# The second layer's modulation vectors as VectorE dot products in the first layer's feed-forward part, in place of fp32 matrix products in its attention part

## The chip, the cores and the metric

One core of one Trainium2 chip runs the whole program, which is launched once. The metric is the device time of that core in microseconds, a median over runs. Engines are named as in the profile: PE is TensorE's matrix product, PEld its weight load, DVE is VectorE, ACT is ScalarE, SP is SyncE, whose queue issues all the DMAs of this kernel.

## What is computed

Two blocks of two layers each run one after the other on 256 tokens of width 1024 in fp32. The change lies in the first block, a diffusion-style transformer with a second stream of 256 context tokens. Per layer, a conditioning vector is turned into six modulation vectors of 1024 numbers, once for the tokens (from `c`) and once for the context (from `c_ctx`):

```python
silu_c, silu_cc = silu(c), silu(c_ctx)
for l in range(2):
    mod_x = silu_c  @ w_ada[l] + b_ada[l]        # w_ada[l]: 1024 x 6144
    mod_c = silu_cc @ w_ada[l] + b_ada[l]
    sh1, sc1, gt1, sh2, sc2, gt2 = split(mod, 6)  # of each
    h = rms_norm(x, g1) * (1 + sc1) + sh1          # tokens and context
    ... three kinds of attention on h @ w_in ...
    x = x + gt1 * (concat(oa, ob, oc) @ w_out[l])
    h2 = rms_norm(x, g2) * (1 + sc2) + sh2
    x = x + gt2 * conv_ffn(h2)
    # the context is updated in the same way, in layer 0 only
```

In layer 1 the context only gives keys and values, so of its six vectors only sh1 and sc1 are used there.

## The kernel before, in words

Products of activations with weights are made of three fp32r products (`mm3`, L175 to L180): each operand is split into a high and a low half, and high by high, high by low and low by high are added up in PSUM. A weight piece of 128x1024 is loaded as `wraw` (L144), copied to a high half `wh` by ACT (L259), and DVE subtracts to get the low half `wl` (L260). PE needs both halves, so PE waits for DVE when DVE is behind.

The modulation of a layer is `ada(l)` (L305). It works in 24 steps: 3 groups of 2048 outputs, 8 steps of 128 rows of `w_ada` each. A step loads two pieces of 128x1024 and makes four plain fp32 products of 128x512 (L318) with the conditioning columns as the stationary operand; four of the 128x32 column groups of PE are used, one for each 512 outputs. After 8 steps DVE adds the bias (L323), PE transposes the row to columns (`ada_cols`, L343), DVE copies the columns out, and the two groups with gates are written to DRAM, from where `gate_rows` (L365) reads each gate back as a row for all partitions.

`ada` is a generator. `tick` (L336) takes one step of it, and `layer` (L747) calls `tick` at the products with `w_in` (`chunk`, L771) and once per head or head pair in the attention (L599, L646). In layer 0 the generator is `ada(0)` followed by `ada(1)` (L754): 8 steps of `ada(0)` run before the first norm, and the other 16 of `ada(0)` and all 24 of `ada(1)` during the attention; what is left is taken at L844.

Layer 0 then goes on: out-projection (`out_proj`, L722), the norm of both streams (`norm_to`, L843), and the feed-forward part (L847 to L864). That has three parts of 8, 7 and 7 hidden tiles. `ffn_up` (L705) makes one tile: two weight pieces, 48 products of 128x512, a convolution of three taps on ACT (L698) and DVE (L701, L702, once for each of two halves), a gate (L716, L717) and a split (L259, L260). Then the down-projection of the part runs, in two halves of the output, with DVE adding the gated result to `x` (L681, L682).

A scheduler decides where each instruction stands on its engine: the order of the source gives it priorities, and independent instructions are moved forward into places where an engine would wait. So the `ada` products stand between the score and output products of the attention. Each engine then runs its own list strictly in order.

Of the kernel before, what the change touches and what calls it, by code (L numbers as in the profile page):

```python
# [12 lines left out]
F32 = mybir.dt.float32  # L13
# [37 lines left out]
class Core:  # L51
    def __init__(self, ctx, tc):
# [20 lines left out]
                  ta32=(64, 4), tb32=(64, 4), nlam=(1, 2), gsubs=(64, 2), raw=(512, 3), rpb=(512, 1), bada=(512, 1))  # L73
# [208 lines left out]
class Block1:  # L282
# [52 lines left out]

    def tick(self):  # L336
        next(self.side, None)
# [21 lines left out]
    def gate_rows(self, l, n, s):  # L359

        K = self.K
        out = K.xo()
        for j in range(2):
            a = 2 * (2 * (n - 1) + j) + s
            self.nc.sync.dma_start(out[:, j * 512 : j * 512 + 512], self.rows[l, n][a : a + 1, :].to_broadcast([P, 512]))  # L365
        return out
# [380 lines left out]
    def layer(self, l):  # L747
# [5 lines left out]
        if l == 0:  # L753
            self.side = chain(*(self.ada(i) for i in range(self.depth)))  # L754
            front = [K.normed(self.x[0]), None]
            for _ in range(KD):
                self.tick()
        else:
            front = [None, None]
# [87 lines left out]
        if full:  # L847
            parts = [range(0, 8), range(8, 15), range(15, 22)]
            for part in parts:
                F = {}  # L850
                for j in part:
                    F[j] = self.ffn_up(l, j, XT, n)
                for cc in range(2):
                    ps = K.acc4()
                    for a in range(part[0], part[-1] + 1, 4):
                        nf = min(4, part[-1] + 1 - a)
                        get = K.weights(f"w1_{l}", "w_down", l, a, nf, [cc * 512], 512)
                        for t in tts:
                            for f in range(nf):
                                j = a + f  # L860
                                K.mm3(ps[t], (F[j][0][:, t * P : t * P + P], F[j][1][:, t * P : t * P + P]), get(f * 512, 512),
                                      j == part[0], j == part[-1])
                    for t in tts:
                        self.add_gated(self.x[t // 2][t % 2][:, cc * 512 : cc * 512 + 512], ps[t], gates[t // 2][:, cc * 512 : cc * 512 + 512])  # L864
        else:
# [592 lines left out]
def _pack(inputs, specs):  # L1458
# [10 lines left out]
    for key, layer, k0, nk, starts, width, piece in specs:  # L1469
        if (key, layer) not in done:  # L1470
            w = inputs["w_in_2" if key == "w_kr_2" else key][layer]
# [63 lines left out]
```

## Time and profile before

| | before |
|---|---|
| median of 3 runs | 2169.36 us (2168.35 to 2172.04) |
| the profiled execution's own time | 2168.22 us |
| span in its trace | 2166.4 us |
| PE busy | 2081.5 us, 96% |
| PEld busy | 1850.0 us, 85% |
| DVE busy | 1493.9 us, 69% |
| ACT busy | 1075.5 us, 50% |
| mean granted TensorE clock | 0.978 of 2.4 GHz |

By stage of layer 0 in the trace: the attention with its products with `w_in` from 34 to 327 us, the out-projection to 377, the norm to 396, the feed-forward part to 757. Layer 1 of the first block has its attention from 832 to 938 us. The busy time of an engine is a union of its instructions; a window's number in brackets is a count of instructions. "PEclk" is the mean clock that was granted in the stretch, as a share of 2.4 GHz.

### The profile page before, as it was taken

Reading aid. Unit: us, or ns where it says so; the run is one execution under the profiler, and the core shown is the slowest. Engines: PE = TensorE matmul, PEld = TensorE weight load, DVE = VectorE, ACT = ScalarE, POOL = GpSimd, SP = SyncE. Lnnn points to the kernel's source line nnn. Section 1 sums busy time; section 2 is a strip of 40 time slices with the busy share of each in tenths; the row PEclk is TensorE's granted clock in tenths of the full one; section 3 lists DMA queues with packets and bytes.
Section 4 is the critical chain, followed back from the end, with each engine's and each line's share of the span. In section 5 each row is a group of like instructions: output and inputs, shape, how many; then the busy total and the mean of one; then the engine's idle time right before and its main releaser. Section 6 shows DMA issues by size and latency. Waiting matters only on the chain.

```text
span 2166.4 us, 35861 instructions
## 1 busy us (share of the span) xinstructions
PE 2081.5 (96%) x14228; PEld 1850.0 (85%) x14228; DVE 1493.9 (69%) x3008; ACT 1075.5 (50%) x1837; POOL 0.8 (0%) x7
## 2 busy tenths in 40 slices
PE   6999999899999999989999999989998999998998
PEld 3886859688888898879997899979997899997997
DVE  5664666755555688687778799775556879876554
ACT  4545552542424366656556644454445644454443
POOL 0000000000000000000000000000000000000000
PEclk9999999899999999999999999999999999999999
DMA  8345563414142321145553555645553455654552
GB/s 341 122 164 180 202 218 116 156 58 146 55 138 67 128 89 55 39 135 199 197 190 132 165 178 182 196 156 171 189 185 123 156 166 163 197 187 139 188 183 72
DMA packets 94840, 331.65 MB, mean 153 GB/s; under 512 B 10928, under 2 KB 11312, under 8 KB 94544
## 3 DMA queue, kind: packets, MB, share of 16 engines
q1 hardware_dynamic: 94672, 329.35, 45.8%
q8 instruction: 112, 1.84, 0.3%
q14 instruction: 56, 0.46, 0.1%
HBM read 328.20 MB, written 1.11 MB: 152 GB/s over the span
## 4 chain that ended last, share of the span: by engine, by line
PE 90%; DVE 6%; ACT 2%; DMA 1%; issue 1%; DVEq 0%; ACTq 0%
PE ps L178 17%; PE ps L179 17%; PE ps L180 17%; PE acc L178 6%; PE acc L179 6%; PE acc L180 6%; PE ada L318 3%; PE ps L525 2%; PE o L566 2%; PE ps L550 2%; PE ada L180 1%; PE ada L178 1%; PE ada L179 1%; PE o L178 1%; PE o L179 1%; PE o L180 1%
## 5 line engine op out<-in xcount | busy, mean ns | idle before, releaser
L178 PE MATMUL ps<-T,wh 128*128 128x256 f32 (+1 forms) x2640 | 787.6, 299 | 1.1 <-ACT T L262 1.1
L179 PE MATMUL ps<-T,wh 128*128 128x256 f32 (+1 forms) x2640 | 785.6, 298 | 0.4 <-DVE T L263 0.4
L180 PE MATMUL ps<-T,wl 128*128 128x256 f32 (+1 forms) x2640 | 784.6, 298 | 0.0
L260 DVE TENSOR_TENSOR wl<-wraw,wh 128x1024 fp32r<-128x1024 f32 (+1 forms) x514 | 608.5, 1200 | 151.0 <-ACT wh L259 83.7
L259 ACT CAST wh<-wraw 128x1024 fp32r<-128x1024 f32 (+1 forms) x514 | 515.9, 1032 | 236.7 <-PE ps L179 77.3
L178 PEld LDWEIGHTS ps<-T,wh 128*128 128x128 f32 x2640 | 506.2, 192 | 18.5 <-ACT T L262 2.2
L179 PEld LDWEIGHTS ps<-T,wh 128*128 128x128 f32 x2640 | 506.5, 192 | 17.3 <-DVE T L263 1.2
L180 PEld LDWEIGHTS ps<-T,wl 128*128 128x128 f32 x2640 | 506.2, 192 | 13.7
L178 PE MATMUL acc<-wh,T 128*128 128x256 f32 (+1 forms) x988 | 314.9, 320 | 4.3 <-ACT T L265 3.1
L179 PE MATMUL acc<-wl,T 128*128 128x256 f32 (+1 forms) x988 | 313.6, 318 | 1.9 <-DVE wl L260 1.9
L180 PE MATMUL acc<-wh,T 128*128 128x256 f32 (+1 forms) x988 | 312.0, 317 | 0.3 <-DVE T L269 0.3
L178 PEld LDWEIGHTS acc<-wh,T 128*128 128x128 f32 x988 | 191.5, 194 | 20.9 <-ACT T L265 3.5
L180 PEld LDWEIGHTS acc<-wh,T 128*128 128x128 f32 x988 | 190.7, 193 | 14.6 <-DVE arena L268 1.7
L179 PEld LDWEIGHTS acc<-wl,T 128*128 128x128 f32 x988 | 191.4, 194 | 13.0 <-DVE wl L260 2.4
L1132 DVE SCALAR_TENSOR_TENSOR arena<-arena 128x241 f32<-128x241 f32 (+14 forms) x240 | 113.1, 473 | 3.7
L259 ACT CAST T<-arena 128x256 fp32r<-128x256 f32 (+2 forms) x128 | 58.8, 468 | 96.2 <-PE ps L179 25.8
L534 DVE TENSOR_REDUCE arena<-ps 128x1 f32<-128x512 f32 (+1 forms) x100 | 67.0, 683 | 44.9 <-PE ps L525 44.5
L318 PE MATMUL ada<-wraw,arena 128*32 128x512 f32 x384 | 86.5, 622 | 11.0 <-DVE arena L293 8.4
L1340 DVE TENSOR_TENSOR arena<-arena,ps 128x256 f32<-128x256 f32 x44 | 18.5, 421 | 113.8 <-ACT arena L1339 113.8
L260 DVE TENSOR_TENSOR T<-arena,T 128x256 fp32r<-128x256 f32 (+2 forms) x128 | 63.1, 500 | 48.6 <-ACT T L259 48.2
L698 ACT ACTIVATE arena<-ps,arena 128x512 f32<-128x512 f32 (+1 forms) x88 | 58.8, 669 | 74.6 <-PE ps L180 74.6
L1339 ACT ACTIVATE arena<-ps 128x256 f32<-128x256 f32 x44 | 16.9, 384 | 156.4 <-PE ps L180 156.4
(226 smaller groups left out, 2316.1 us busy)
## 6 DMA issues: line engine op xcount, KB each, us to landing
wraw<-w SPq DMA_DIRECT2D x586, 512.0 KB, 4.1
wraw<-w SPq DMA_DIRECT2D x22, 256.0 KB, 3.4
xo<-row SPq DMA_DIRECT2D x12, 256.0 KB, 5.7
v<-xin SPq DMA_DIRECT2D x4, 512.0 KB, 7.9
arena<-rpb SPq DMA_DIRECT2D x8, 256.0 KB, 3.5
v<-post SPq DMA_DIRECT2D x4, 512.0 KB, 4.0
arena<-bada SPq DMA_DIRECT2D x6, 256.0 KB, 6.9
arena<-bc SPq DMA_DIRECT2D x2, 768.0 KB, 4.0
```

The costliest lines, as they stand in the source:

```text
L178: mm(out, ah, bh, start=start, stop=False)
L179: mm(out, ah, bl, start=False, stop=False)
L180: mm(out, al, bh, start=False, stop=stop)
L259: a = nc.scalar.copy(h, src)
L260: b = nc.vector.tensor_tensor(l, src, h.bitcast(F32), op=ALU.subtract)
L318: nc.tensor.matmul(ps[32 * g : 32 * g + 32, :], self.cT[:, k].rearrange("p s r -> p (s r)"), raw[g // 2][0][:, g % 2 * 512 : g % 2 * 512 + ...
L525: self.nc.tensor.matmul(ps[:, col : col + 256], a[:, c], b, start=(n == 0), stop=(n == len(q[s]) - 1))
L534: nc.vector.tensor_reduce(m, ps.rearrange("p (t k) -> p t k", t=nt), axis=AX, op=ALU.max, negate=True)
L550: nc.tensor.transpose(ps[:, b * P : b * P + P], p[:, b * P : b * P + P], K.ident)
L566: self.nc.tensor.matmul(out[64 * i : 64 * i + 64, t * P : t * P + P], v[:, k, cols[i] : cols[i] + 64], pts[i][:, b * P : b * P + P], start ...
L698: nc.scalar.activation(y[:, :n], ps[:, :n], AF.Identity, scale=cw[:, j, 1:2], bias=self.sm["cb"][:, j : j + 1])
L1132: yield v.scalar_tensor_tensor(y[:, lo:hi], zs[j][:, lo + t - 15 : hi + t - 15], self.cfw[:, j, t : t + 1], y[:, lo:hi], op0=ALU.mult, op1 ...
```

## The change

Layer 1's modulation is no longer made by `ada`. `w_ada[1]` is sent transposed, so that an output stands on a partition and its 1024 weights lie along the free axis. `crows` loads the two conditioning vectors as one row pair for all partitions (1 MB) and takes their silu on ACT. `ada_dots` has 48 steps, one for each 128 outputs: a step loads one piece of 128x1024, and DVE multiplies it by the conditioning row and sums along the row in one instruction (`scalar_tensor_tensor` with `accum_out`; the product itself goes to a tile `unread`). For sh1 and sc1, the first 16 steps, it does so twice, once for each stream, for the others once: 64 such instructions. After each 8 steps a small add puts the bias on, and for the scales the gain. The two gates are written to DRAM as columns and read back as one row each.

The steps are ticked in layer 0's feed-forward part: two after each up-tile, one after each half of a down-projection, 50 places for 48 steps. `ada(0)` stays as it was, and its 16 later steps still run in the attention.

```diff
-                  ta32=(64, 4), ..., raw=(512, 3), rpb=(512, 1), bada=(512, 1))
+                  ta32=(64, 4), ..., raw=(512, 3), rpb=(512, 1), bada=(512, 1), badac=(48, 1), adav=(48, 2), crow=(2048, 1), unread=(1024, 1))
...
+    def crows(self):
+        K, nc = self.K, self.nc
+        self.crow = K.tile([P, 2, D], F32, "crow")
+        nc.sync.dma_start(self.crow, self.ap["crow"].partition_broadcast(P))
+        nc.scalar.activation(self.crow, self.crow, AF.Silu)
+        self.badac = K.tile([P, 48], F32, "badac")
+        nc.sync.dma_start(self.badac, self.ap["badac"])
...
+    PARTS = dict(sh1=0, sc1=8, gt1=16, sh2=24, sc2=32, gt2=40)
+    def ada_dots(self, l):
...
+        vals = [K.tile([P, 48], F32, "adav") for _ in range(2)]
+        for name, b0 in self.PARTS.items():
+            streams = (0, 1) if name in ("sh1", "sc1") else (0,)
+            for b in range(b0, b0 + 8):
+                ((w, _),) = K.raw(f"w1_{l}", "w_ada_t", l, b, 1, [0], D)
+                for s in streams:
+                    nc.vector.scalar_tensor_tensor(K.tile([P, D], F32, "unread"), w, 1.0, self.crow[:, s], op0=ALU.mult, op1=ALU.mult,
+                                                   accum_out=vals[s][:, b : b + 1])
+                if b == b0 + 7:
+                    for s in streams:
+                        self.part(l, name, s, vals[s][:, b0 : b0 + 8], self.gn[:, l])
+                yield
+    def part(self, l, name, s, v, gn):
...
+        nc.vector.tensor_tensor(v, v, self.badac[:, b0 : b0 + 8], op=ALU.add)
+        if name[:2] == "gt":
+            row = self.rows[l, int(name[2])] = K.dram.tile([1, D], F32, name=f"row_{l}_{name}_{s}")
+                nc.sync.dma_start(row.rearrange("o (b p) -> p (o b)", p=P), v)
+            return
...
     def gate_rows(self, l, n, s):
+        if l > 0:
+            self.nc.sync.dma_start(out, self.rows[l, n].to_broadcast([P, D]))
+            return out
...
         if l == 0:
-            self.side = chain(*(self.ada(i) for i in range(self.depth)))
+            self.side = self.ada(0)
...
         if full:
+            self.crows()
+            self.side = self.ada_dots(l + 1)
             parts = [range(0, 8), range(8, 15), range(15, 22)]
...
                     F[j] = self.ffn_up(l, j, XT, n)
+                    self.tick()
+                    self.tick()
...
+                    self.tick()
                     for t in tts:
                         self.add_gated(...)
+            for _ in self.side:
+                pass
```

Lines move with the new code. In the lists of the changed kernel below, L359 is the new dot product, L572, L597 and L691 are the scores, transposes and outputs of the attention (L525, L550 and L644 before), L748, L749 and L764 the convolution and gate of an up-tile (L701, L702 and L717 before).

PE's list in the last attention of layer 0 (`attend_c`), before. `ada` are the modulation products, `o` and `ps` the attention's.

```order
L318 MATMUL ada_2498<-wraw_2991,arena 32x512 x2
L550 MATMUL ps_2908<-arena 128x128 x4
L644 MATMUL o_2917<-v_294_2838,arena 128x64 x4
L550 MATMUL ps_2940<-arena 128x128 x4
L318 MATMUL ada_2498<-wraw_3020,arena 32x512
L644 MATMUL o_2917<-v_294_2838,arena 128x64 x4
```

The same place of the changed kernel; `acc` are sums of the out-projection, which stood behind the attention before.

```order
L178 MATMUL acc_3170<-wh_3175,T_2141 128x256
L179 MATMUL acc_3170<-wl_3176,T_2141 128x256
L180 MATMUL acc_3170<-wh_3175,T_2141 128x256
L691 MATMUL o_2823<-v_271_2744,arena 128x64 x4
L178 MATMUL acc_3170<-wh_3175,T_2141 128x256
L572 MATMUL ps_2920<-T_2752,T_2536 128x256
L572 MATMUL ps_2920<-T_2778,T_2536 128x256
```

In the places that the `ada` products left, the scheduler put products of later stages; in the first attention of this stretch (`attend_ab`) these are the products of the next `w_in` chunk. Some 135 such products stand inside `attend_c` now, and some 73 inside `attend_ab`.

DVE's list in the norm before the feed-forward part, before: the end of the first stream's splits (L268, L269), and the scaling (L232) of the second stream's last tile.

```order
L269 TENSOR_TENSOR T_3914<-arena,T_3914 128x256
L201 SCALAR_TENSOR_TENSOR arena<-arena 128x1
L355 SCALAR_TENSOR_TENSOR arena<-ps_4074,arena 128x8
L202 SCALAR_TENSOR_TENSOR arena<-arena 128x1
L965 TENSOR_SCALAR arena<-arena 128x124
L232 TENSOR_SCALAR xo_3986<-v_310_2901,arena 128x512
```

The same place of the changed kernel:

```order
L359 SCALAR_TENSOR_TENSOR arena<-wraw_4016,arena 128x1024
L269 TENSOR_TENSOR T_3712<-arena,T_3712 128x256
L200 SCALAR_TENSOR_TENSOR arena<-arena 128x1
L359 SCALAR_TENSOR_TENSOR arena<-wraw_4020,arena 128x1024
L201 SCALAR_TENSOR_TENSOR arena<-arena 128x1
L359 SCALAR_TENSOR_TENSOR arena<-wraw_4020,arena 128x1024
L202 SCALAR_TENSOR_TENSOR arena<-arena 128x1
L232 TENSOR_SCALAR xo_3784<-v_287_2807,arena 128x512
```

Five dot products now stand in the norm: two between the first stream's scalings and its splits, and these three ahead of the last scaling of the second stream. Three more stand ahead of the norm, among the out-projection's adds, and one ahead of the norm's last split.

DVE's list in the first part of up-tiles, before: two convolutions, a gate, a split of a tile and two weight splits.

```order
L701 SCALAR_TENSOR_TENSOR arena<-ps_4172,arena 128x2x255
L702 SCALAR_TENSOR_TENSOR arena<-ps_4172,arena 128x2x255
L260 TENSOR_TENSOR T_4157<-arena,T_4157 128x512
L260 TENSOR_TENSOR wl_4315<-wraw_4308,wh_4314 128x1024
L260 TENSOR_TENSOR wl_4384<-wraw_4379,wh_4383 128x1024
L701 SCALAR_TENSOR_TENSOR arena<-ps_4200,arena 128x2x255
L702 SCALAR_TENSOR_TENSOR arena<-ps_4200,arena 128x2x255
L717 TENSOR_TENSOR arena<-arena 128x512
```

The same of the changed kernel:

```order
L748 SCALAR_TENSOR_TENSOR arena<-ps_4117,arena 128x2x255
L260 TENSOR_TENSOR wl_4274<-wraw_4269,wh_4273 128x1024
L749 SCALAR_TENSOR_TENSOR arena<-ps_4117,arena 128x2x255
L359 SCALAR_TENSOR_TENSOR arena<-wraw_4342,arena 128x1024
L260 TENSOR_TENSOR wl_4278<-wraw_4271,wh_4277 128x1024
L748 SCALAR_TENSOR_TENSOR arena<-ps_4145,arena 128x2x255
L359 SCALAR_TENSOR_TENSOR arena<-wraw_4342,arena 128x1024
L749 SCALAR_TENSOR_TENSOR arena<-ps_4145,arena 128x2x255
L359 SCALAR_TENSOR_TENSOR arena<-wraw_4346,arena 128x1024
L764 TENSOR_TENSOR arena<-arena 128x512
L359 SCALAR_TENSOR_TENSOR arena<-wraw_4346,arena 128x1024
```

From the first convolution of the first part to the last convolution of its eighth tile, 24 dot products stand on DVE between the 32 convolutions, 8 gates, 8 tile splits and 15 weight splits. The other 31 of the 64 follow in the down-projections and the second and third part.

## Rows read from the trace of the kernel before

**Rows 1.** The page: busy time by engine, and the chain that ended last.
```profile
PE 2081.5 (96%) x14228; PEld 1850.0 (85%) x14228; DVE 1493.9 (69%) x3008; ACT 1075.5 (50%) x1837; POOL 0.8 (0%) x7
...
PE 90%; DVE 6%; ACT 2%; DMA 1%; issue 1%; DVEq 0%; ACTq 0%
```
**Rows 2.** Windows of layer 0; us, busy us of PE, PEld, DVE, ACT, POOL, PEclk, DMA share, GB/s.
```profile
163.00:231.00 68.00, 67.48 (x498) 40.38 (x498) 35.03 (x88) 36.93 (x95) 0.00 (x0) 0.98 0.55 183
231.00:273.00 42.00, 42.00 (x365) 40.12 (x366) 25.98 (x80) 22.17 (x44) 0.00 (x0) 1.00 0.62 216
273.00:327.50 54.50, 53.22 (x306) 27.63 (x304) 33.40 (x114) 30.14 (x85) 0.00 (x0) 1.00 0.63 213
...
377.00:396.30 19.30, 10.38 (x54) 7.60 (x54) 16.64 (x64) 13.50 (x29) 0.00 (x0) 0.61 0.68 219
396.30:484.00 87.70, 87.70 (x384) 72.23 (x383) 57.20 (x77) 41.48 (x55) 0.00 (x0) 0.99 0.24 78
484.00:526.00 42.00, 42.00 (x187) 34.77 (x186) 19.68 (x24) 9.29 (x10) 0.00 (x0) 1.00 0.37 126
526.00:736.00 210.00, 210.00 (x928) 173.89 (x927) 125.53 (x175) 80.39 (x102) 0.00 (x0) 1.00 0.32 102
```
**Rows 3.** Windows of L318 alone: us, PE busy, PEld busy, PEclk, DMA share, GB/s.
```profile
192.50:231.00 38.50, 14.75 (x64) 2.04 (x64) 1.00 0.58 195
231.00:273.00 42.00, 2.13 (x16) 0.31 (x16) 1.00 0.62 216
273.00:326.00 53.00, 26.29 (x96) 3.58 (x96) 1.00 0.63 213
```
**Rows 4.** Groups of instructions, 163 to 231 us: busy us, mean ns, idle before.
```profile
L318 PE MATMUL ada<-wraw,arena 128*32 128x512 f32 x102 | 22.3, 610 | 0.0
...
L343 PE MATMUL ps<-arena 128*128 128x128 f32 x4 | 0.7, 286 | 0.0
```
**Rows 5.** Windows of layer 1's attention, where no modulation product runs; columns as in rows 2.
```profile
832.00:888.00 56.00, 55.69 (x493) 47.81 (x493) 43.31 (x115) 38.57 (x90) 0.00 (x0) 1.00 0.15 48
888.00:906.00 18.00, 15.92 (x144) 15.60 (x144) 10.81 (x34) 12.22 (x25) 0.00 (x0) 1.00 0.26 89
906.00:938.00 32.00, 29.95 (x222) 28.56 (x221) 24.54 (x77) 20.75 (x51) 0.00 (x0) 0.89 0.15 42
```
**Rows 6.** Groups, 832 to 888 us: products of other stages between the attention's.
```profile
L178 PE MATMUL acc<-wh,T 128*128 128x256 f32 x34 | 10.0, 296 | 0.0
```
**Rows 7.** Timeline of PE around the norm: start us, us, instruction, idle before and its releaser.
```profile
377.17 1.92 PE L318 MATMUL ada<-wraw,arena 128*32 128x512 f32 x16
382.13 4.53 PE L236 MATMUL ps<-arena,xo 128*128 128x128 f32 x20 [3.04 <-DVE xo L232]
...
394.71 1.97 PE L236 MATMUL ps<-arena,xo 128*128 128x128 f32 x8 [2.99 <-DVE xo L232]
396.33 1.20 PE L178 MATMUL ps<-T,wh 128*128 128x512 f32 x2
```
**Rows 8.** Timeline of DVE in the norm.
```profile
383.70 0.69 DVE L323 TENSOR_TENSOR arena<-ada,arena 128x512 f32<-128x512 f32 x1
385.16 0.54 DVE L268 TENSOR_SCALAR arena<-ps,arena 128x256 f32<-128x256 f32 x1 [0.77 <-ACT T L265]
```
**Rows 9.** Groups on DVE, whole program, by shape: busy us, mean ns, idle before.
```profile
L260 DVE TENSOR_TENSOR wl<-wraw,wh 128x1024 fp32r<-128x1024 f32 x494 | 595.2, 1221 | 148.1 <-ACT wh L259 83.7 <-PE ps L180 27.5 <-issue 12.5
...
L701 DVE SCALAR_TENSOR_TENSOR arena<-ps,arena 128x510 f32<-128x510 f32 x44 | 32.8, 745 | 22.9 <-ACT arena L698 22.9
L701 DVE SCALAR_TENSOR_TENSOR arena<-ps,arena 128x255 f32<-128x255 f32 x44 | 21.1, 481 | 23.8 <-ACT arena L698 23.8
...
L633 DVE SCALAR_TENSOR_TENSOR arena<-arena 128x512 f32<-128x512 f32 x16 | 11.9, 743 | 0.1
...
L201 DVE SCALAR_TENSOR_TENSOR arena<-arena 128x1 f32<-128x1 f32 x30 | 6.1, 215 | 0.5
```
**Rows 10.** DMA issues of the page: KB each, median us to landing.
```profile
wraw<-w SPq DMA_DIRECT2D x586, 512.0 KB, 4.1
```
**Rows 11.** Timeline of ACT near 42 us, and a table load of the feed-forward part.
```profile
41.97 1.05 ACT L259 CAST wh<-wraw 128x1024 fp32r<-128x1024 f32 x1
47.69 0.59 ACT L451 COPY arena<-acc 128x512 f32<-128x512 f32 x1 [4.68 <-PE acc L180]
...
L716 ACT ACT_TABLE_LOAD x1 | 1.3, 1283 | 1.8 <-DVE arena L702 1.8
```

More of the change, by code (lines that the diff above doesn't have):

```diff
@@ L72 @@
     RINGS1 = dict(cT=(256, 1), gn=(32, 1), sm1=(SM1N, 1), mod=(8, 24), gs64=(64, 2), gs32=(32, 2), ta64=(128, 4), tb64=(128, 4),
-                  ta32=(64, 4), tb32=(64, 4), nlam=(1, 2), gsubs=(64, 2), raw=(512, 3), rpb=(512, 1), bada=(512, 1))
+                  ta32=(64, 4), tb32=(64, 4), nlam=(1, 2), gsubs=(64, 2), raw=(512, 3), rpb=(512, 1), bada=(512, 1), badac=(48, 1), adav=(48, 2), crow=(2048, 1), unread=(1024, 1))
     RINGS2 = dict(cfwh=(124, 1), gatebh=(32, 1), gmws=(512, 1), bc2=(BC2N, 1), cfz=(512, 2), cfy=(256, 4), scz=(512, 1), gate=(512, 4), merge=(512, 2), gv=(512, 2), kr=(512, 1))
@@ L334, in ada @@
             yield
+    def crows(self):
[7 more added lines that the diff above has]
+    def ada_dots(self, l):
+        K, nc = self.K, self.nc
+        m = self.mod[l] = {}
+        vals = [K.tile([P, 48], F32, "adav") for _ in range(2)]
[11 more added lines that the diff above has]
+    def part(self, l, name, s, v, gn):
+        K, nc = self.K, self.nc
+        b0 = self.PARTS[name]
+        nc.vector.tensor_tensor(v, v, self.badac[:, b0 : b0 + 8], op=ALU.add)
+        if name[:2] == "gt":
+            row = self.rows[l, int(name[2])] = K.dram.tile([1, D], F32, name=f"row_{l}_{name}_{s}")
+            with nc.allow_non_contiguous_dma(reason="a column to a row"):
+                nc.sync.dma_start(row.rearrange("o (b p) -> p (o b)", p=P), v)
+            return
+        if name[:2] == "sc":
+            nc.vector.scalar_tensor_tensor(v, v, 1.0, gn[:, 0:8] if name == "sc1" else gn[:, 8:16], op0=ALU.add, op1=ALU.mult)
+        self.mod[l].setdefault("a" + name[2] if name[:2] == "sc" else name, []).append(v)
     def tick(self):
@@ L1470, in _pack @@
         if (key, layer) not in done:
-            w = inputs["w_in_2" if key == "w_kr_2" else key][layer]
+            w = inputs[{"w_kr_2": "w_in_2", "w_ada_t": "w_ada"}.get(key, key)][layer]
+            if key == "w_ada_t":
+                w = w.T
             done[key, layer] = w[:, perms[key]] if key in perms else w
@@ L1503 @@
     arrays["gn"] = np.stack([np.concatenate([_cols(i["g_norm1"][l], KD), _cols(i["g_norm2"][l], KD)], axis=1) for l in range(2)], axis=1)
-    arrays["bada"] = np.stack([np.repeat(i["b_ada"][l].reshape(3, 4, 1, 512), 32, axis=2).reshape(3, P, 512) for l in range(2)])
+    arrays["bada"] = np.stack([np.repeat(i["b_ada"][l].reshape(3, 4, 1, 512), 32, axis=2).reshape(3, P, 512) for l in range(1)])
+    arrays["badac"] = _cols(i["b_ada"][1], 48)
+    arrays["crow"] = np.concatenate([i["c"][0], i["c_ctx"]])
     arrays["rpb"] = np.stack([_rpb_tiles(i["rpb_b"][l]) for l in range(2)])
```

## The prediction

> **What bounds the kernel now.** I read the page first: PE is busy 96% of the span, and 90% of the chain that ended last is PE work [rows 1]. So a microsecond of PE work that leaves counts, unless PE only did it where it would have waited. Next come the windows of layer 0, since both the place that loses work and the place that gains it lie there [rows 2]. From 163 to 327.5 us, the attention, PE is busy 67.48 of 68, 42 of 42 and 53.22 of 54.5 us: 1.8 us idle in 164.5. In the feed-forward part (396.3 to 736 us) PE is never idle, and DVE, which is to take the work, is busy 57.2 of 87.7 us in the first eight up-tiles, 19.68 of 42 in the down-projection behind them and 125.53 of 210 in the rest. Between the two stands the norm, 19.3 us with PE busy 10.38 and a clock of 0.61 of full speed (so part of it at 1.2 GHz) but DVE busy 16.64: there DVE sets the pace. The products that go are in the windows of L318 alone [rows 3]. All times are of the profiled execution, 2168.22 us, which is 1.1 us below the median of 2169.36.
>
> **What goes.** The 24 steps of `ada(1)` run from 192.5 us on. They take 14.75, 2.13 and 26.29 us of PE, together 43.2 us [rows 3], in stretches in which PE is full [rows 2]. The two transposes to columns in these stretches add 2 x 0.7 [rows 4]: 44.5 us. The last 1.92 us of `ada(1)`, at 377.17, stand in a gap in which PE waits for DVE anyway [rows 7], and count as nothing; so does the third transpose.
>
> **How much comes back as waiting.** The `ada` products had no one to wait for and filled the holes between softmax steps. In their place the scheduler has put 73 products of the next chunk and 135 of the out-projection. A product of 512 columns takes 87.7 / 384 = 0.228 us [rows 2], so one of 256 columns about 0.114, and the 208 make 24 us of filling against 43 us that left. Whether that is enough is read from layer 1's attention, which never had modulation products: 56, 18 and 32 us with 0.31, 2.08 and 2.05 us idle, and a clock of 0.89 in the last [rows 5], which is 3.5 us of full-speed time lost. That is 8 us in 106. There the filling was also chunk and out-projection work, 3 x 34 products in the first window [rows 6]. Layer 0 has two streams, so twice the products to stand behind in the chunks (42 us without a hole now). I take 5 us more waiting than now, between 0 and 8.
>
> **What a dot product costs.** The trace has no DVE instruction with a sum as a second output. The same instruction without it takes 481 ns for 255 columns and 745 for 510 [rows 9], 1.04 ns a column, so 1.28 us for 1024. Reading out the sum I price like the smallest DVE instruction, 0.2 us (215 ns) [rows 9]: 1.45 us together, and 64 of them are 93 us of DVE. From below stands the plain subtraction of the same size, 1.22 us [rows 9]; from above, twice the extrapolated rate and the read, 2.75 us. I take 1.45, since L633, with both inputs fp32 in SBUF as here, takes 743 ns for 512 columns and so shows no second pass [rows 9].
>
> The Trainium skill (Vector Engine (DVE) Microarchitecture Reference, Points that are easy to get wrong) says that this instruction with two non-bf16 SBUF sources runs at half throughput, because both read ports are taken and none is left for reading back the accumulator. By L633 that is not so without a sum; with one no row here shows it, and what would follow is the second rival below.
>
> **The first eight tiles.** 24 dot products at 1.45 are 34.8 us; DVE's free time there is 87.7 - 57.2 = 30.5 us [rows 2]. DVE falls 4.3 us behind by the end. What PE needs of DVE are the low halves of the weights, and the list has these split two tiles ahead at the start, some 20 us; the down-projection that follows leaves DVE 22.3 us free to catch up [rows 2]. So PE should hardly see it: 1 us, between 0 and 7. The other 31, 45 us, face 22.3 + 84.5 us of free DVE and cost nothing. If that cover went, each dot product would cost its full 1.45 us.
>
> **The norm.** Five dot products stand in a stretch that DVE sets: 5 x 1.45 = 7.3 us. The bias add that they replace there took 0.69 us [rows 8], and some of the first one falls in the 0.77 us in which DVE waited for ACT [rows 8]. Behind the delayed scaling PE waited 2.99 us for DVE already [rows 7], and the first up-tile waits for these transposes. I take +5.5 us, between 2 (only the last three count, partly) and 8 (the two pieces that they read are loaded just then, 4.1 us to landing [rows 10], and DVE waits in order). The three ahead of the norm stand where DVE waits for PE.
>
> **The head.** The silu of the rows is put on ACT near 42 us, with a table load of 1.28 us before it and one more before the first softmax [rows 11]; for 2048 columns it takes about 2 us, twice the 1.05 of a 1024-column copy. The 1 MB load ahead of it delays the ACT queue at most until it lands. ACT was idle for 4.68 us right there [rows 11], so what is left is mainly the second table load: 1.5 us, between 0 and 4.
>
> **Transfers.** The weights of `ada(1)` are the same 48 pieces as before, moved. In the first eight tiles the queue loads four pieces of 512 KB per tile of 11 us, 190 GB/s; in the 231 to 273 window it moved 216 [rows 2] with PE full. The two gate columns written to DRAM hold up the SP queue until their bias add is done; loads behind them run well ahead of their use. I count nothing, and leave 2 us in the upper bound.
>
> **The sum.** -44.5 + 5 + 1 + 5.5 + 1.5 = -31.5 us. From 2169.4 that is **2138 us**. With all low ends it is -44.5 + 2 = -42.5, with all high ends -44.5 + 8 + 7 + 8 + 4 + 2 = -15.5: 2127 to 2154.
>
> **The rivals.** *The softmax, not PE, sets the attention.* Then the products only sat in holes and removing them returns little. Layer 1 gives a cadence: 24 head steps in 56 us [rows 5] against 24 in 68 us here [rows 2], with 22.3 us of L318 in the latter [rows 4]. So 22.3 us of products cost 12, and the 14.75 that go would return 7.9; the last window has 8 steps in 32 us there, 12 in 54.5 here: 48 against 54.5, 6.5 back. With 2.1 in the chunks and 1.4 for transposes 18 us come back, less 8 in norm, head and tiles: 2159 us. Against it: the 56 us of layer 1 hold 102 products of other stages [rows 6], about 12 us, so they are full too and not a softmax limit.
>
> The Trainium skill (Trainium Kernel Development and Optimization, Performance Expectations) calls matmul busy time a poor measure, because matmuls are pipelined, and points to the weight loads' share. By that share the windows here are the emptier ones, 40.38 of 68 us for PEld against 47.81 of 56 in layer 1 [rows 2, 5], which would speak for holes behind the fp32 products; the page's measure does not say whether other work can enter them.
>
> *The dot product is much slower than the row says.* At price p, norm and first part cost 5p + 24p - 30.5 - 1.8 us, with 6.5 in head and waiting; against 44.5 this turns to a loss at p = (44.5 - 6.5 + 32.3) / 29 = 2.42 us. At 2.75 it is +9.5 us: **2179 us, slower**. For it: nothing in the trace shows the instruction with a sum. Against it: L633.
>
> *The loads come late.* DVE's list is in order, so a late piece of `w_ada` stops the weight splits behind it. At 183 GB/s, as in the first window [rows 2], the 2.1 MB of a tile take 11.5 us, 0.5 more than PE: 4 us in eight tiles, 2142 us. It is the same sign, and inside the bounds.
>
> **How the numbers follow.** The full saving with its bounds, the late loads included, gets 0.80; the softmax case 0.13; the slow dot product 0.07. The range leaves out half of each tail: 2126 to 2157 holds the first case and about half of the second. A measurement of this kernel tells 0.2%, 4.3 us, from no change; below 2165 lie the first two cases and above 2173.7 the third at 2.75 us. A price near 2.42 would be no change. So faster 0.91, same 0.04, slower 0.05.
>
> **What would show it.** Right: the windows from 163 to 377 us shortened by some 40 us in all, with PE still above 95%; no L318 after 190 us; 64 of the new instruction at 1.3 to 1.5 us with its read; a norm gap of 24 to 25 us in place of 19.1 (377.2 to 396.3); a feed-forward part of layer 0 within 5 us of its length now. Wrong: PE idle of over 10 us in the attention (first rival); new instructions above 2 us and PE waiting for `wl` in the first eight tiles (second); DVE waiting for `wraw` there (third).

## The result, and the profile after

| | before | after |
|---|---|---|
| median | 2170.29 us (2168.35 to 2172.04, 4 runs) | 2130.28 us (2127.15 to 2131.59, 4 runs) |
| profiled execution, its span | 2168.22, 2166.4 us | 2131.49, 2129.7 us |

The ratio is 0.9814, with a 95% interval of 0.9801 to 0.9826: 40 us faster, where 31.5 were forecast (2138, in a range of 2126 to 2157). Measured again later, the kernel after gave 2130.53 us (2129.55 to 2131.15) against 2170.03 before.

The page of the kernel after, busy time and chain, to be held against [rows 1]:

```profile
PE 2039.0 (96%) x14024; PEld 1845.4 (87%) x14024; DVE 1556.4 (73%) x3136; ACT 1076.5 (51%) x1840; POOL 0.8 (0%) x7
...
PE 90%; DVE 6%; ACT 2%; issue 1%; DMA 1%; DVEq 0%; SPq 0%; ACTq 0%
```

PE lost 42.5 us of busy time and VectorE took on 62.5. PE's share stays at 96%, so the share tells nothing of what happened. The windows by stage do (kernel after; columns as in [rows 2]): the two parts of the attention with the chunk between them, the out-projection, the norm, and the feed-forward part in three pieces.

```profile
168.00:229.40 61.40, 61.33 (x502) 46.28 (x501) 39.76 (x96) 41.66 (x101) 0.00 (x0) 0.98 0.39 130
229.40:262.00 32.60, 31.93 (x279) 31.54 (x279) 23.05 (x74) 18.91 (x42) 0.00 (x0) 1.00 0.17 56
262.00:309.20 47.20, 45.54 (x332) 43.52 (x333) 36.97 (x121) 31.39 (x87) 0.00 (x0) 0.89 0.12 39
309.20:339.55 30.35, 30.35 (x253) 30.14 (x252) 29.68 (x80) 6.60 (x11) 0.00 (x0) 1.00 0.45 160
339.55:361.85 22.30, 7.40 (x32) 6.32 (x33) 20.84 (x70) 12.80 (x28) 0.00 (x0) 0.61 0.36 118
361.85:450.00 88.15, 88.15 (x384) 72.54 (x383) 82.77 (x132) 40.35 (x54) 0.00 (x0) 0.98 0.46 155
450.00:492.00 42.00, 42.00 (x187) 34.80 (x186) 21.74 (x28) 10.02 (x11) 0.00 (x0) 1.00 0.43 146
492.00:722.82 230.82, 230.81 (x1019) 190.85 (x1017) 169.74 (x265) 85.73 (x115) 0.00 (x0) 1.00 0.54 171
```

The first four windows, the attention with its out-projection, are 171.6 us long together, and PE is idle for 2.4 us of them. The granted clock is 0.89 of full speed in the third, where the kernel before had 1.00 in its last attention window [rows 2]. In the first eight tiles VectorE is busy 82.77 of 88.15 us (57.20 of 87.70 before) and PE has no hole.

Each stage's length, from the starts and ends of PE's rows in the timelines, for all kernels that ran (the names are explained below). "Second chunk" ends with the second set of products with `w_in`, at 155.9 us before; "attention" goes on to the last product of the out-projection.

| us | first product | to end of second chunk | attention | norm and feed-forward | layer 1 | second block |
|---|---|---|---|---|---|---|
| before | 33.8 | 122.1 | 221.3 | 379.5 | 196.4 | 1204.0 |
| after | 36.1 | 124.1 | 179.4 | 383.3 | 194.0 | 1203.5 |
| after, again | 34.2 | 124.2 | 179.4 | 383.1 | 195.0 | 1202.5 |
| neither | 34.6 | 123.9 | 179.6 | 377.9 | 197.1 | 1205.2 |
| place | 34.0 | 121.9 | 179.5 | 409.6 | 194.9 | 1203.2 |
| halves | 34.1 | 121.9 | 179.6 | 432.1 | 197.5 | 1205.2 |
| both | 35.9 | 123.7 | 221.8 | 384.9 | 195.3 | 1203.2 |
| fence | 36.4 | 123.6 | 179.5 | 382.5 | 195.1 | 1203.5 |
| twice | 34.1 | 124.1 | 179.1 | 409.6 | 195.3 | 1203.5 |
| spread | 36.6 | 121.4 | 179.2 | 379.6 | 195.0 | 1202.5 |
| late row | 34.6 | 121.7 | 179.3 | 379.6 | 195.0 | 1202.5 |
| late row, again | 34.8 | 122.6 | 179.6 | 380.0 | 194.1 | 1203.7 |
| more | 37.8 | 128.1 | 205.8 | 378.4 | 193.9 | 1202.5 |
| chunks | 34.7 | 121.2 | 188.4 | 378.8 | 196.1 | 1203.6 |

The attention gave 42.0 us in both profiles of the kernel after. Given back were 3.6 to 3.8 us in the norm and feed-forward part, 2.0 to 2.1 before 160 us, and 0.5 to 2.3 ahead of the first product. The last two columns are products that no edit changes, and they differ by up to 3.6 and 2.7 us between executions, where the attention without `ada(1)` repeats within 0.5 us in ten of them (179.1 to 179.6): a profile tells the attention to some tenths, but the whole only to some 3 us.

### The profile page after: what moved, and what is told of

It is laid out like the page before. It is cut to its first block, busy times and chain, and to the rows that moved or that the text cites. A ratio compares the mean times of both kernels' runs of the same rounds, so it can differ in the third digit from the quotient of the medians.

```text
span 2129.7 us, 35607 instructions
## 1 busy us (share of the span) xinstructions
PE 2039.0 (96%) x14024; PEld 1845.4 (87%) x14024; DVE 1556.4 (73%) x3136; ACT 1076.5 (51%) x1840; POOL 0.8 (0%) x7
## 4 chain that ended last, share of the span: by engine, by line
PE 90%; DVE 6%; ACT 2%; issue 1%; DMA 1%; DVEq 0%; SPq 0%; ACTq 0%
PE ps L178 17%; PE ps L179 17%; PE ps L180 17%; PE acc L178 7%; PE acc L179 6%; PE acc L180 6%; PE ps L572 2%; PE o L613 2%; PE ps L597 2%; PE ada L318 2%; PE ada L180 1%; PE ada L179 1%; PE ada L178 1%; PE o L180 1%; PE o L179 1%; PE o L178 1%
## 5 line engine op out<-in xcount | busy, mean ns | idle before, releaser
L180 PEld LDWEIGHTS ps<-T,wl 128*128 128x128 f32 x2640 | 506.6, 192 | 13.7
L260 DVE TENSOR_TENSOR T<-arena,T 128x256 fp32r<-128x256 f32 (+2 forms) x128 | 63.1, 501 | 36.6 <-ACT T L259 36.2
L359 DVE SCALAR_TENSOR_TENSOR arena<-wraw,arena 128x1024 f32<-128x1024 f32 x64 | 78.0, 1219 | 13.7 <-DMA wraw<-w 13.7
L236 PE MATMUL ps<-arena,xo 128*128 128x128 f32 x176 | 38.2, 386 | 50.9 <-DVE xo L232 30.0
```

The lines of the kernel that those rows point to most:

```text
L180: mm(out, al, bh, start=False, stop=stop)
L260: b = nc.vector.tensor_tensor(l, src, h.bitcast(F32), op=ALU.subtract)
L359: nc.vector.scalar_tensor_tensor(K.tile([P, D], F32, "unread"), w, 1.0, self.crow[:, s], op0=ALU.mult, op1=ALU.mult, accum_out=vals[s][:, ...
```

## Experiments

**Neither, place, both, fence.** Four kernels, to price the removal, the addition, the place and the norm apart.

Neither: no modulation for layer 1, anywhere.

```diff
-            self.side = self.ada_dots(l + 1)
+            self.side = iter(())
+            b, g = self.badac, self.gn[:, 1]
+            self.mod[1] = dict(sh1=[b[:, 0:8]] * 2, a1=[g[:, 0:8]] * 2, sh2=[b[:, 24:32]], a2=[g[:, 8:16]])
...
```

> Layer 1's modulation is left out altogether: no fp32 products in the attention, no dot products in the feed-forward part (layer 1 reads the biases and gains alone in its place); the rows' load and silu stay. My theory: the 64 dot products lie under PE's work and cost only what they add to the norm before the feed-forward part, so this is 3 to 6 us below the changed kernel's 2130, about 2125, with the norm at 16 to 18 us in place of 22.3 and the feed-forward part at 360 to 361 us as before. Rival one, that the dots and their loads also take PE time in the feed-forward part or slow other transfers: 10 us or more below, under 2120, with a feed-forward part that is shorter than 360.

Measured: 2127.35 us (2124.29 to 2129.14). The dots as built cost 2.9 us by the medians, just under my 3 to 6, and 5.2 to 5.4 by the stage in which they stand (377.9 against 383.1 and 383.3). My theory holds: the dots, 78 us of VectorE's busy time (the window under "The price of a dot product"), nearly vanish under PE. The same stage is 1.6 us shorter than before the change, so the end of `ada(1)`, which stood in the norm, had cost something too.

Place: the fp32 products stay, but are ticked in the feed-forward part.

```diff
-            self.side = chain(*(self.ada(i) for i in range(self.depth)))
+            self.side = self.ada(0)
...
+            self.side = self.ada(1)
                     F[j] = self.ffn_up(l, j, XT, n)
+                    self.tick()
+                    if j in (8, 15):
+                        self.tick()
```

> The fp32 products of layer 1's modulation stay on PE, but their 24 steps are taken in the feed-forward part of layer 0 (one at each up-tile, two at the first of the second and third part) and not in its attention; no dot products. My theory: what counts is that PE's work leaves PE, not the place: the attention gets some 42 us shorter, the feed-forward part some 45 us longer, and the time is that of the kernel before, 2166 to 2173 us. Rival one, that the place was the fault (the products held up the softmax chain): about 2130 to 2140, the changed kernel's time. Rival two, that the attention is bound by the softmax and the fp32 products sat in holes there: only some 18 us come back in the attention, 45 are paid, about 2195.

Measured: 2154.30 us (2153.71 to 2156.80), ratio 0.9930 (0.9915 to 0.9945). No theory had this. The attention gets 41.8 us shorter as expected, but the norm and feed-forward part only 30.1 longer: the same products cost far less there. L318 alone is busy 24.93 us there and 43.2 in the attention before [rows 3], for the same 176 records (the windows under "halves"). The timeline of PE in the kernel before shows why (a product makes two records, so a step of four makes eight):

```profile
283.34 1.04 PE L318 MATMUL ada<-wraw,arena 128*32 128x512 f32 x2
284.31 1.10 PE L644 MATMUL o<-v,arena 128*128 128x64 f32 x8
285.35 1.06 PE L318 MATMUL ada<-wraw,arena 128*32 128x512 f32 x6
...
291.10 1.05 PE L318 MATMUL ada<-wraw,arena 128*32 128x512 f32 x4
```

One product alone takes 1.04 us, two take 1.05, three 1.06. In the feed-forward part of the run "place" all four stand together and take the same:

```profile
402.76 1.06 PE L318 MATMUL ada<-wraw,arena 128*32 128x512 f32 x8
```

So a step costs one 1.05 us for each group of neighbouring products, however many of its four are in it. It isn't a fixed price for changing to these products and back: two whole steps next to one another take 1.92 us (x16, at 377.17 in [rows 7]), so the second step, with all four products, adds 0.86. On PE's list before, the 24 steps of `ada(1)` stand in 42 groups, since attention products came between; in "place" in 24. The Trainium skill (TensorEngine Tiling (Array Packing), Key Properties) says that tiles of the array are independent and can run in parallel. The trace agrees for neighbours (1.06 us for four against 1.04 for one), and shows that it ends with the next product that isn't one of them. That reading was put to a test of its own, "halves", below.

Both: `ada(1)` in the attention as before, and the dots too, with results that nobody reads.

```diff
-            self.side = self.ada(0)
+            self.side = chain(*(self.ada(i) for i in range(self.depth)))
```

> Both at once: layer 1's modulation by fp32 products in the attention as in the kernel before, which layer 1 uses, and the dot products with their loads in the feed-forward part, whose results nobody reads. My theory: the addition alone costs the norm (3 to 7 us more than the 19.1 us before), the silu of the rows in the head (0 to 4 us) and nothing in the feed-forward part: 2174 to 2181 us, 4 to 11 us above the kernel before. Rival one, that the dots cost much more and the attention gave back more than 42 us: 2185 or more. Rival two, that the addition is free and 42 us is not the whole of what the attention gives back: within 2 us of 2170.

Measured: 2175.89 us (2172.71 to 2178.36), ratio 1.0024 (1.0016 to 1.0033): the addition costs 5.0 us, as my theory had it, 5.4 of it in the norm and feed-forward part. Against the kernel after, `ada(1)` is the one difference: 45.6 us.

Fence: every dot is ordered behind the norm's last split on VectorE.

```diff
-                    nc.vector.scalar_tensor_tensor(...)
+                    ins = nc.vector.scalar_tensor_tensor(...)
+                    K.queue(ins, self.after[1])
...
+            self.after = K.fence
```

> The changed kernel with one thing more: every dot product is put behind the norm's last split on VectorE, so that none stands in the norm or ahead of it. My theory: the norm's gap falls from 22.3 us to 15.5 to 18 us and the eight displaced dots (8 x 1.3 us) find room in the first down-projection, so 4 to 6 us below the changed kernel, 2124 to 2126 us. Rival: the first eight tiles have no room for 32 dots (32 x 1.3 = 42 us against 30.5 us free), PE then waits for low halves of weights there, and the gain is lost again: 2129 to 2137 us with PE idle in the feed-forward part.

Measured: 2129.72 us (2127.35 to 2131.82): no gain, the rival. PE's first product of the feed-forward part comes 12.0 us after the out-projection in place of 22.3, then PE waits for the rest of the splits until 16.7 us. So the norm is 5.6 us shorter, as in my theory, but norm and feed-forward part together only 0.5 to 0.7. Windows of the fenced run, first tiles and down-projection, and its first 10 us of the feed-forward part with those of the kernel after below:

```profile
356.18:444.00 87.82, 87.16 (x368) 70.88 (x369) 84.06 (x134) 38.70 (x50) 0.00 (x0) 0.97 0.47 162
444.00:490.00 46.00, 44.23 (x193) 35.68 (x192) 29.94 (x43) 9.59 (x12) 0.00 (x0) 1.00 0.44 154
356.18:366.00 9.82, 9.82 (x31) 7.93 (x32) 8.33 (x18) 3.79 (x6) 0.00 (x0) 0.70 0.01 2
```

```profile
361.85:372.00 10.15, 10.15 (x39) 7.93 (x38) 10.15 (x21) 7.54 (x12) 0.00 (x0) 0.84 0.08 18
```

VectorE is busy 84.06 of 87.82 us, and PE stands idle for 0.66 + 1.77 us, for low halves of weights: with the eight displaced dots there are 32 in the first tiles, and the room is used up. Another part of the loss is the granted clock of the first tile, 0.70 in place of 0.84. By these rows that is some 1.3 us of full-speed time, an estimate; the rest is not told apart.

**Halves, twice, spread, more.** Halves takes "place" and ticks each step in two pairs.

```diff
+                    if l == 1 and g == 1:
+                        yield
...
+            if l == 0:
+                for _ in range(2 if j in (8, 15) else 1):
+                    self.tick()
             ys.append(self.conv(...))
```

> As the run with the fp32 products in the feed-forward part (2154.3 us), but each step's four products in two pairs, some 24 products of the up-tile apart; the same products, loads and stage. Theory of the groups: the four products of a step stand on four column groups of PE and run side by side, 1.06 us for the four, and a pair that stands apart takes as long as the four; so 24 pairs more by 1.06 us: 25 us more, 2175 to 2182 us. Rival, that a product costs by its size wherever it stands: 2152 to 2157, as the run before.

Measured: 2178.07 us (2176.18 to 2181.53), 23.8 us above "place", inside the theory's bounds. Windows of L318 alone (columns as in [rows 3]), "place" first, then "halves":

```profile
354.00:750.00 396.00, 24.93 (x176) 3.83 (x176) 0.99 0.45 151
```

```profile
355.00:750.00 395.00, 43.45 (x176) 5.79 (x174) 0.99 0.43 145
```

The same 176 records, 22 of the 24 steps, take 24.93 and 43.45 us, in 21 and 41 groups. This settles it: 18 us of the 43 that `ada(1)` took in the attention were due to its products standing apart. The stage as a whole grew by 22.5 us; the 4 us beyond are not in L318's own busy time, and no run tells them apart.

Twice: each dot is done two times.

```diff
...
+                    nc.vector.scalar_tensor_tensor(..., accum_out=vals[2][:, b : b + 1])
```

> The changed kernel with each dot product done twice (the second into a column that nobody reads), so a price of 2.6 us for one in place of 1.3; same loads. The prediction's own arithmetic (5 in the norm and 24 in the first eight tiles count, less 30.5 us of room) gives 29 x 1.3 = 38 us more, 2168 us, near no change against the kernel before; with the lead of the weight splits hiding 10 to 20 us of it, 2148 to 2158. Rival, that VectorE's room in the whole feed-forward part (some 146 us) takes the second half too and only the norm feels it: 2136 to 2140.

Measured: 2158.45 us (2157.01 to 2161.99), 28.2 above the kernel after. PE's waits in the first 140 us of the feed-forward part of this run (engine, line waited for; us in total, times, longest):

```profile
PE ps L180 <- DVE wl L260: 9.4, 4, 4.4
PE acc L179 <- DVE wl L260: 8.7, 3, 8.1
```

This is the second rival's mechanism: VectorE late with the low halves, 18.1 us of waiting. The norm itself grew by 0.5 us only (22.8 against 22.3), so its dots did not count twice as the 29 x 1.3 = 38 us had it. What else the stage lost (409.6 against 383.3 us) agrees with the granted clock behind the norm and around these waits: 0.73 in the first 12 us and 0.91 from 450 to 510 us, against 0.85 and 1.00 in the kernel after, some 8 us of full-speed time by these figures, an estimate. A second dot adds 1.23 us of busy time, so by these two points the time rises by 28.2 / 1.23 = 23 us for each us of price. On a straight line, which no third point tests, the change would turn to a loss at about 1.23 + 40 / 23 = 3 us, not at 2.42.

Spread: the fence, the silu of the rows also behind the norm, and fewer dots in the first part.

```diff
-        nc.scalar.activation(self.crow, self.crow, AF.Silu)
+        ins = nc.scalar.activation(self.crow, self.crow, AF.Silu)
+        K.queue(ins, self.after[0])
... (the fence as above)
-                    self.tick()
-                    self.tick()
+                    for _ in range(1 if part[0] == 0 else 2 if part[0] == 8 else 3):
+                        self.tick()
```

> The changed kernel with the dot products behind the norm's last split, the silu of the rows behind the norm on ScalarE (its table is then the one that the first up-tile loads), and the steps spread: one after each up-tile of the first part, two in the second, three in the third, so 16 dots in the first eight tiles in place of 24. My theory: the norm at 16.7 us as in the fenced run, the feed-forward part back at 361 us, the head 1 us less: 2121 to 2125 us, 5 to 9 below the changed kernel. Rival, that what the norm gives back is lost in the first up-tile whatever stands behind it (its weights or the clock): 2128 to 2131.

Measured: 2125.33 us (2124.15 to 2126.18), ratio 0.9794 (0.9780 to 0.9807), just above my theory's upper end. Norm and feed-forward part take 379.6 us, 2.9 less than in the fenced run, 1.7 more than without any dots. With 16 dots in the first eight tiles the room nearly holds (PE waits 1.15 us near their start), and PE is busy through the later stretch in which it waited in the fenced run:

```profile
444.00:490.00 46.00, 46.00 (x205) 38.10 (x204) 28.09 (x39) 10.36 (x11) 0.00 (x0) 1.00 0.48 166
```

The other 2.7 us came back before 160 us, mostly not by ScalarE's time. L318 alone, from the first product with `w_in` on, kernels before, after and spread:

```profile
33.76:192.50 158.74, 27.27 (x128) 3.69 (x128) 0.96 0.48 167
```

```profile
36.09:200.00 163.91, 30.45 (x128) 4.08 (x128) 0.96 0.48 173
```

```profile
36.64:200.00 163.36, 27.75 (x128) 3.78 (x128) 0.96 0.49 176
```

The same 128 records of layer 0's own `ada(0)`. On PE's list its 16 later steps stand in 24 groups before, 27 after, 25 in the spread run. The silu among ScalarE's work moved the scheduler's places by a little, and three groups more were split, 1.05 us each, two of them before the end of the second chunk. All runs with these products in the same places of the source agree: that stretch has 18 groups in the six profiles with the silu in the head (both of after, neither, both, fence and twice: 123.6 to 124.2 us in the table), and 16 in the six without it there (before, place, halves, spread and both of late row: 121.4 to 122.6).

More: layer 0's gates and second shift and scale as dots too (32 steps, 64 dots), in the attention.

```diff
-            self.side = self.ada(0)
+            self.side = chain(islice(self.ada(0), KD), self.ada_dots(0))
```

> As the spread kernel, and layer 0's own modulation too, but for its first third (shift and scale of the first norm), as dot products: 32 steps with both streams, 64 dots, taken in layer 0's products with w_in and its attention, in place of 16 fp32 steps; the silu of the rows is back in the head. Theory: some 27 us of fp32 products leave PE, and VectorE, busy under 60% there, has room for 83 us: 12 to 25 us below the spread kernel, 2098 to 2112 us. Rival: VectorE's list is in order, so dots and the loads that they wait for hold up the softmax and the weight splits in the attention, and the gain is lost: 2120 us or more with PE idle for VectorE from 36 to 340 us.

Measured: 2154.68 us (2149.30 to 2157.67), 29 us worse than spread, although the 27.75 us of L318 above left PE: the rival. The attention takes 205.8 us in place of 179.2. The longest waits of PE from 36 to 372 us, and a window, of this run:

```profile
PE ps L550 <- ACT xo L525: 10.8, 3, 6.5
PE ps L596 <- DVE arena L632: 7.9, 1, 7.9
PE ps L550 <- DVE xo L512: 6.1, 5, 3.3
```

```profile
165.00:200.00 35.00, 21.77 (x140) 19.56 (x139) 33.84 (x95) 17.41 (x38) 0.00 (x0) 0.71 0.41 142
```

In the spread run VectorE is busy 20.38 us in this window and PE all 35. Here PE waits for normed queries and keys (L512, L525). VectorE's timeline shows what holds them up (L361 is the dot, L209 to L211 are steps of the norm's reciprocal root):

```profile
170.79 0.15 DVE L209 TENSOR_TENSOR arena<-arena 128x4 f32<-128x4 f32 x1
170.86 1.22 DVE L361 SCALAR_TENSOR_TENSOR arena<-wraw,arena 128x1024 f32<-128x1024 f32 x1
172.00 0.08 DVE L361 DVE_READ_ACCUMULATOR arena<-wraw,arena 128x1 f32 x1
172.00 0.16 DVE L211 SCALAR_TENSOR_TENSOR arena<-arena 128x4 f32<-128x4 f32 x1
172.08 0.15 DVE L210 SCALAR_TENSOR_TENSOR arena<-arena 128x4 f32<-128x4 f32 x1
172.15 1.22 DVE L361 SCALAR_TENSOR_TENSOR arena<-wraw,arena 128x1024 f32<-128x1024 f32 x1
173.30 0.08 DVE L361 DVE_READ_ACCUMULATOR arena<-wraw,arena 128x1 f32 x1
173.30 0.16 DVE L209 TENSOR_TENSOR arena<-arena 128x4 f32<-128x4 f32 x1
```

Behind every one or two steps of 0.15 us stands a dot of 1.2 us. The chain that PE waits for is made of such small steps, and the gaps between them took the dots. My "under 60%" was also read from single windows; over the whole stretch the spread run has

```profile
36.00:340.00 304.00, 295.39 (x2336) 255.03 (x2336) 220.89 (x641) 171.36 (x383) 0.00 (x0) 0.97 0.37 131
```

so VectorE is busy 220.89 of 304 us, 73%, and 78 us of dots would have had to fill nearly every gap of the 83 us left. The granted clock is 0.71 in the window above, 0.91 in the spread run's.

**Late row, chunks.** Late row takes spread and puts the 1 MB row load behind the gate rows' loads on SP's queue.

```diff
-        nc.sync.dma_start(self.crow, ...)
+        ins = nc.sync.dma_start(self.crow, ...)
+        K.queue(ins, self.gate_dma)
...
```

> As the spread kernel (2125.3 us), with the 1 MB load of the conditioning rows put behind the first gate row's loads on SP's queue, out of the loads of the first 36 us. My theory: the first product with w_in, at 35.9 to 36.6 us in four of the runs that load the rows there and 33.8 to 34.1 in the three that don't, comes back to 34 us, so 2 us less, 2122 to 2125 us. Rival, that the spread of these starts is chance (two runs with the load start at 34.1 and 34.6): no change, 2125 to 2127, and a first product at 35 to 36.6 us.

Measured: 2125.24 us (2123.83 to 2128.51), no change. The first product stands at 34.6 us, but the runs with the early load have it anywhere from 34.1 to 36.6 (and 37.8 in "more"), the others from 33.8 to 34.8. About 1 us on the mean is likely; it isn't shown.

Chunks: on top of that, `ada(0)`'s 16 steps only at the products with `w_in`, two at each, none at the heads.

```diff
             self.pv_pair(self.o, self.pts, v, vcols[g : g + 2], unit)
-            self.tick()
+            pass
...
             if name != "qb":
                 self.tick()
+                self.tick()
...
```

> As the run with the late row load, and the 16 later steps of layer 0's own fp32 modulation are all taken at the products with w_in, two at each, none at the heads of the attention; same products. By the finding on the groups: its four-group products stand on PE in 18 places in place of 27, 9 x 1.05 us less, 2112 to 2117 us. Rival, that the steps filled holes of the softmax that now stay empty, or that their loads, 2 MB for each pair, come late in these stretches: 2122 us or more, with PE idle between 80 and 120 or 160 and 220 us.

Measured: 2135.63 us (2130.37 to 2137.00), 10 us worse. In the 227 us from 34 us on, L318 does fall from 27.9 to 22.8 us, but the attention takes 188.4 us in place of 179.3. PE is idle for 11.3 us of it in place of 4.4, and most of the difference lies from 231 to 309 us, the second half of the attention, later than the rival had it. The rival's time holds, and its first reading, that the products had filled holes between softmax steps, fits; no wait for a load shows. But 3.4 us are a single wait for the modulation's own bias add, which now comes late, so the fillers are not the whole of it.

**Once more, side by side.**

> The changed kernel once more, beside the run with spread dots and late rows, on the same chip. Theory: 2128 to 2132 us as at first, 40 us below the kernel before; the norm at 22.3 us, and with a start of the first product between 34 and 36.6 us the second pair of stages (80 to 160 us) as long as at first.

> The run with spread dots and late rows once more, beside the changed kernel. Theory: 4 to 6 us below it, 2123 to 2127 us; no overlap of the two groups of times. Rival, that the 5 us are a difference between chips: within 2 us of the changed kernel.

Measured on one chip: 2130.53 us (2129.55 to 2131.15) and 2125.70 us (2123.30 to 2125.95). So the late-row version beats both kernels, the changed one by 5 us, with no overlap; the rival of a difference between chips falls.

## Why the prediction was right, point by point

**What goes, and the waiting that comes back.** The last L318 starts before 193 us, and only layer 0's are left. Forecast -44.5 + 5 for the attention; measured -42.0, so 2.5 us came back in place of 5. It did not come back as idle time. The whole stage, before and after (columns as in [rows 2]):

```profile
155.90:377.24 221.34, 216.99 (x1584) 160.12 (x1587) 135.70 (x394) 105.23 (x250) 0.00 (x0) 0.98 0.52 175
```

```profile
160.20:339.55 179.35, 175.99 (x1396) 156.28 (x1395) 134.89 (x393) 104.22 (x250) 0.00 (x0) 0.95 0.27 92
```

PE is idle for 4.35 us before and 3.36 after, but the granted clock fell from 0.98 to 0.95. By these figures that is 9 us of full-speed time in place of 4, an estimate. The forecast's 5 us held both kinds, as layer 1 shows both [rows 5]. Direction and size hold, and "both" against the kernel after prices the same products at 45.6. What the prediction did not see is why they cost 43 us: it took L318's busy time as the work itself. 18 us of it belong to the place; in the feed-forward part the same work costs 25. Part of the gain was to be had without any dot product, as "place" shows: 16 us by the medians, 11.7 by its two stages (-41.8 + 30.1). The last 1.92 us of `ada(1)`, counted as nothing, were not quite that: "neither" is 1.6 us shorter than the kernel before in norm and feed-forward part.

**The softmax rival.** It said that 18 us would come back. The attention gave 42.0, and PE is idle for 2.4 us of 171.6. It falls.

**The price of a dot product.** Forecast 1.45 us; the trace of the kernel after has two instructions for it:

```profile
L359 DVE SCALAR_TENSOR_TENSOR arena<-wraw,arena x64: 1212/1218/1229, 323.3 to 649.7; 128x1024 f32<-128x1024 f32 x64
L359 DVE DVE_READ_ACCUMULATOR arena<-wraw,arena x64: 79/82/88, 324.5 to 650.8; 128x1 f32 x64
...
  DMA wraw<-w: 13.7, 12
```

That is 1.22 us, the plain subtraction's 1221 ns of [rows 9], and 0.08 for the read: 1.30 as a sum of durations. But the records overlap with their neighbours, and all 128 are busy for 78.48 us together, 1.23 a dot (window of L359 alone: us, VectorE busy, PEclk, DMA share, GB/s):

```profile
320.00:652.00 332.00, 78.48 (x128) 0.97 0.52 170
```

The Trainium skill (Vector Engine (DVE) Microarchitecture Reference, Points that are easy to get wrong) has this form with two non-bf16 SBUF sources at half throughput; the trace disagrees for fp32, with the sum as without: the form takes no longer than the subtraction of the same size. The second rival's price falls; its mechanism is real ("twice"), with the break-even nearer 3.

**The first eight tiles and the late loads.** Forecast +1; PE has no hole there, and the whole feed-forward part behind the norm is 0.4 to 0.6 us longer. VectorE's dots did wait for `wraw`, 13.7 us in 12 waits, but not where I had listed that as a mark of the third rival: one wait of 1.4 us falls into the first eight tiles, at their very end, one of 0.2 us ahead of the norm, and the other ten come after 470 us. VectorE waited in time that it had there, and PE felt nothing (230.81 of 230.82 us busy).

**The norm.** Forecast +5.5, a gap of 24 to 25 us; measured 22.3, in both profiles, so +3.2. The mechanism shows in the timelines of VectorE and PE:

```profile
355.54 1.22 DVE L359 SCALAR_TENSOR_TENSOR arena<-wraw,arena 128x1024 f32<-128x1024 f32 x1
...
357.08 1.22 DVE L359 SCALAR_TENSOR_TENSOR arena<-wraw,arena 128x1024 f32<-128x1024 f32 x1
...
358.36 1.22 DVE L359 SCALAR_TENSOR_TENSOR arena<-wraw,arena 128x1024 f32<-128x1024 f32 x1
...
359.69 0.48 DVE L232 TENSOR_SCALAR xo<-v,arena 128x512 f32<-128x512 f32 x1
```

```profile
360.24 1.97 PE L236 MATMUL ps<-arena,xo 128*128 128x128 f32 x8 [8.34 <-DVE xo L232]
```

Three dots stand ahead of the last scaling, and PE waits 8.34 us for it where it waited 2.99 [rows 7]. The five dots are 5 x 1.23 = 6.2 us; what they replaced was more than the one bias add. The small modulation adds L355 went as well, and VectorE's short waits for ScalarE shrank, from 2.2 us in the gap before to 1.4 after. So the term that was too large is the net price of the five dots, 3.2 us in place of 5.5.

**The head.** Forecast +1.5 for a table load; measured +2.5 and +4.3 in two profiles. The step that failed is the cause: 2.0 of it is fp32 products of `ada(0)` in more groups, on PE, and it went when the silu moved. The rest, 0.5 and 2.3 us, is ahead of the first product, where the runs scatter, and a price of the table load is not shown.

**The sum.** By stages the two profiles give -36.7 and -38.7; the medians give -40.0. Of the 8.5 us between forecast and medians, 2.5 lie in the waiting, 2.3 in the norm and 0.5 in the first tiles, against which the head took 1 to 2.8 more. 2.8 us are shorter executions of layer 1 and the second block in both profiles, which the change does not touch and which scatter by as much among the other kernels. What is left, 1.3 to 3.3 us, is the difference between profiled executions and medians. So the terms as forecast miss the stages by 2.8 us at most, partly against one another, and how near the total came is in part chance.

## What to carry to other kernels

Before a busy time on PE is counted as work to be saved, look how its products stand: products on different column groups of the array cost one product's time together only as neighbours, so a large part of the price can be the place (here 18 of 43 us). Idle time of VectorE is room only where PE does not wait for the next thing on its list: under a dense stretch of products 78 us of dots all but vanished (3 to 5 us), between the small dependent steps of the attention as many lost 29 us on top of the 28 us of PE work that they saved. When VectorE's work is moved under PE, keep it out of the norm and thin it out where the room is smallest, both at once: out of the norm alone gave the gain back here, and thinning alone was not run.

## What the hardware showed that was not expected

- fp32 products of 128x512 on four column groups of 32: 1.04 us for one alone, 1.06 for three or four neighbours, 1.92 for eight; 176 records take 24.93 or 43.45 us by nothing but what stands between.
- `scalar_tensor_tensor` with a sum, both inputs fp32 in SBUF, 1024 columns: 1.22 us, as fast as a plain subtraction, and 0.08 us for a separate read of the accumulator, which overlaps so far that a dot counts 1.23 us of busy time.
